# Last MLP product of a decoder block done half by half of the tokens, with a final norm behind each half

## The chip, the cores and the metric

The kernel runs on one core of a Trainium2 chip. The metric is the device time of one execution in microseconds; the kernel before takes 736.61 us, the median of 3 runs (735.38 to 737.58). Engines are called as in the profile: PE is TensorE (PEld its weight loads), DVE is VectorE, ACT is ScalarE, POOL is GpSimd, SP issues DMAs.

## The reference, cut to what matters

One decoder block on 512 tokens of width 1024 in float32: a pooling branch and a differential attention branch, gated and projected; cross attention to 256 memory rows; and a squared-ReLU MLP of width 4096. The change touches only the end:

```
hm = rms_norm(x, g_mlp)
x = x + jnp.square(jax.nn.relu(hm @ w_up)) @ w_down
return rms_norm(x, g_final)
```

`rms_norm(x, g)` is `x * rsqrt(mean(x*x) + 1e-6) * g`, the mean over the 1024 features of each token.

## The kernel before, in words

Activations lie transposed: features on the 128 partitions, tokens along the row, so the residual stream `res` is 8 tiles of 128 x 512. A float32 product is made of three matmuls of rounded halves (`mm3`, lines 103 to 106): high x high, high x low, low x high. Each weight block of 128 x 1024 is loaded by SP into `wraw` (3 buffers) and split by `split` (lines 109 to 111): ACT casts the high part (`whi`, 3 buffers, or two of the 4 buffers of `mhl`), DVE subtracts to get the low part. `weights` (lines 207 to 215) loads up to 7 blocks ahead and splits up to 4 ahead in this stage; it walks one list of blocks (`add`, lines 137 to 141 and 323 to 328).

The MLP runs in 4 groups of 1024 hidden features. A group has two `up_set` calls (lines 874 to 914) that make the activations `act[0..7]`, each a pair (high, low) of 128 x 512, by seven block products of a Strassen scheme; then 8 products m = 0 to 7 with w_down (lines 926 to 951), each over k = 0 to 7 and added to `res[m]`. `act[4..7]` come from the second `up_set` late: `act[4]` and `act[5]` share the tile pair called x in `up_set`, `act[6]` and `act[7]` the pair y, and tokens 0 to 255 and 256 to 511 of each are written by separate instructions. The products m = 0 and 1 therefore begin with k = 0 to 3 of both, and take k = 6, 7, 4, 5 of both afterwards.

In the last group each m also squares `res[m]` into the sum `ss3` and writes `res[m] * g_final` to `y3` (`finish`, lines 916 to 920). Product m = 7 is made by halves of the tokens (A is 0 to 255, B is 256 to 511; `last_rows`, lines 825 to 852). Four k steps behind each half comes its `norm`: three matmuls sum the squares over partitions into PSUM, ACT takes Ln and Exp, DVE does one Newton step, and DVE and POOL multiply `y3` by the result (`ON_POOL`: four of eight pieces on POOL for A, three for B), each pair of pieces followed by an output DMA on SP.

PE's instructions stand in the order written. A scheduler sets the order of the other engines, and each engine works through its list in order. `acc` is a PSUM tag of two buffers, `sc` one of three, `tr` one of two; a product that takes a buffer waits until the one before in it has been read.

Of the kernel before, what the change touches and what calls it, by code (L numbers as in the profile page):

```python
# [14 lines left out]
ALU = mybir.AluOpType  # L15
# [34 lines left out]
def block_kernel(ctx: ExitStack, tc: tile.TileContext, x0g, xT, memT, wv, wm, wst, wckv, wpool, vecs, csts, outT):  # L50
# [272 lines left out]
    for g in range(NG):  # L323
        for n in (2 * g, 2 * g + 1):
            for name in FIRST_ORDER if n == 0 else ORDER:
                where[n, name] = add((n, name))
        for m in range(KC):
            where["dn", g, m] = add(wm[WDN + KC * g + m])
# [496 lines left out]
    def last_rows(m, o, c):  # L825

        w = c.stop - c.start
        V.tensor_tensor(res[m][:, c], o[:, c], res[m][:, c], op=ALU.add)
        sq = tmp()[:, :w]
        S.activation(sq, res[m][:, c], AF.Square)  # L830
        S.activation(y3[m // 2][:, 1, c], res[m][:, c], AF.Copy, scale=vec[:, G_FINAL + m:G_FINAL + m + 1])

        def norm():
            s = ps("tr", 2)[:, :w]
            nc.tensor.matmul(s, ones, st["sp3"][0][:, c], start=True, stop=False)
            nc.tensor.matmul(s, ones, st["sp3"][1][:, c], start=False, stop=False)
            nc.tensor.matmul(s, one_f, sq, start=False, stop=True)
            r, v, l = tmp()[:, :w], tmp()[:, :w], tmp()[:, :w]
            with tc.high_priority():
                S.activation(l, s, AF.Ln, bias=eps, scale=1.0 / D)  # L840
                S.activation(r, l, AF.Exp, scale=-0.5)
                V.tensor_scalar(v, s, 1.0 / D, EPS, op0=ALU.mult, op1=ALU.add)
                V.tensor_tensor(l, r, r, op=ALU.mult)
                V.scalar_tensor_tensor(l, l, -0.5, v, op0=ALU.mult, op1=ALU.mult)
                V.scalar_tensor_tensor(r, l, 1.5, r, op0=ALU.add, op1=ALU.mult)
            for j in range(KC // 2):
                for i in range(2):
                    eng = G if 2 * j + i in ON_POOL[c.start > 0] else V
                    eng.tensor_tensor(y3[j][:, i, c], y3[j][:, i, c], r, op=ALU.mult)  # L849
                nc.sync.dma_start(outT[:, 2 * j:2 * j + 2, c], y3[j][:, :, c])  # L850

        after(4, norm)
# [63 lines left out]
    def finish(m, o, last):  # L916
        residual(m, o)
        if last:
# [106 lines left out]
```

## Time and profile before

| what | us |
|---|---|
| median of 3 runs (lowest, highest) | 736.61 (735.38, 737.58) |
| the profiled execution's own time | 736.63 |
| its span, first to last instruction | 734.5 |
| PE busy in the span | 706.9 (96%) |
| DVE busy | 512.8 (70%) |
| ACT busy | 392.6 (53%) |
| mean granted TensorE clock | 0.986 |

All rows come from this one execution. 2.13 us of its time lie outside the span. Busy time of PE includes the overlap of one matmul with the next, so the pace of matmuls is read from the distance of their starts. A row of the timeline gives start, duration, engine, line, what is written and read, shapes, and in brackets how long the engine was idle before and what ended that.

### The profile page before, as it was taken

The numbers are of one execution on the slowest core, as the hardware profiler recorded it, in microseconds if no ns is written. First come the engines' busy times: TensorE is split into PE (matmuls) and PEld (weight loads), VectorE is DVE, ScalarE is ACT, GpSimd is POOL, SyncE is SP. The second block draws the span as 40 slices with busy tenths as digits, with TensorE's granted clock in tenths as the row PEclk, the third lists the DMA queues.
The fourth block names the chain that finished last, engine by engine and source line by source line (L and its number), as shares of the span: only waits on it lengthen the run. The fifth ranks groups of instructions, "written<-read, shape, count | busy, mean of one in ns | idle before, by whom it ended". The sixth has DMA issues, their size and how long they took to land.

```text
span 734.5 us, 10275 instructions
## 1 busy us (share of the span) xinstructions
PE 706.9 (96%) x3960; PEld 613.9 (84%) x3960; DVE 512.8 (70%) x797; ACT 392.6 (53%) x641; POOL 72.7 (10%) x66
## 2 busy tenths in 40 slices
PE   8999999999999999999986999999999999999993
PEld 6877888788889888888876988899889988899882
DVE  7597999875988555663688984489455974489426
ACT  7498998676765433443655651356213651256422
POOL 0043112534000000000000001000000001000003
PEclk9999999999999999999997999999999999999997
DMA  8433223143535532115633645365354645314003
GB/s 320 138 115 115 85 75 114 58 150 109 172 104 182 177 139 87 58 58 167 177 87 116 184 159 123 87 173 192 87 114 144 202 133 125 86 58 144 30 1 114
DMA packets 28112, 91.09 MB, mean 124 GB/s; under 512 B 3072, under 2 KB 5120, under 8 KB 28064
## 3 DMA queue, kind: packets, MB, share of 16 engines
q1 hardware_dynamic: 25712, 81.92, 33.8%
q0 software_dynamic: 2352, 8.52, 6.8%
q8 instruction: 31, 0.51, 0.3%
q14 instruction: 17, 0.14, 0.1%
HBM read 86.24 MB, written 2.10 MB: 120 GB/s over the span
## 4 chain that ended last, share of the span: by engine, by line
PE 80%; DVE 7%; DMA 5%; ACT 4%; issue 2%; POOL 0%; SPq 0%; DVEq 0%; POOLq 0%
PE acc L104 16%; PE acc L106 15%; PE acc L105 15%; PE sc L104 9%; PE sc L106 9%; PE sc L105 9%; DMA wraw<-wst 2%; DMA mraw<-wst 2%; DVE wlo L111 1%; ACT tmp L447 1%; DVE mix L849 1%; DMA tmp<-xT 1%; DVE tmp L445 1%; PE sc L386 1%; ACT tmp L417 1%
## 5 line engine op out<-in xcount | busy, mean ns | idle before, releaser
L110 ACT CAST whi<-wraw 128x1024 fp32r<-128x1024 f32 (+1 forms) x98 | 102.4, 1045 | 119.0 <-PE acc L105 51.8
L104 PE MATMUL acc<-xg,whi 128*128 128x512 f32 x400 | 158.2, 396 | 1.0 <-DVE vr L572 1.0
L106 PE MATMUL acc<-xg,wlo 128*128 128x512 f32 x400 | 156.1, 390 | 0.0
L105 PE MATMUL acc<-xg,whi 128*128 128x512 f32 x400 | 155.8, 390 | 0.0
L111 DVE TENSOR_TENSOR wlo<-wraw,whi 128x1024 fp32r<-128x1024 f32 (+1 forms) x98 | 121.4, 1238 | 26.1 <-ACT whi L110 25.7
L106 PEld LDWEIGHTS acc<-xg,wlo 128*128 128x128 f32 x400 | 75.1, 188 | 16.2
L104 PEld LDWEIGHTS acc<-xg,whi 128*128 128x128 f32 x400 | 75.2, 188 | 16.0 <-ACT whi L110 1.3
L105 PEld LDWEIGHTS acc<-xg,whi 128*128 128x128 f32 x400 | 75.2, 188 | 14.6
L572 DVE TENSOR_TENSOR vr<-acc,vr 128x512 f32<-128x512 f32 x41 | 28.3, 690 | 72.8 <-PE acc L106 72.8
L104 PE MATMUL sc<-mix,whi 128*128 128x256 f32 (+1 forms) x192 | 56.5, 294 | 0.0
L106 PE MATMUL sc<-mix,wlo 128*128 128x256 f32 (+1 forms) x192 | 56.2, 293 | 0.0
L105 PE MATMUL sc<-mix,whi 128*128 128x256 f32 (+1 forms) x192 | 56.2, 293 | 0.0
L885 DVE TENSOR_TENSOR tmp<-sc,tmp 128x512 f32<-128x512 f32 x56 | 37.7, 688 | 8.7 <-PE sc L106 8.5
L110 ACT CAST mhl<-wraw 128x1024 fp32r<-128x1024 f32 x22 | 23.2, 1054 | 35.9 <-PE acc L105 22.2
L105 PE MATMUL acc<-xg,mhl 128*128 128x512 f32 x104 | 40.6, 390 | 0.0
L104 PE MATMUL acc<-xg,mhl 128*128 128x512 f32 x104 | 40.5, 389 | 0.0
L106 PE MATMUL acc<-xg,mhl 128*128 128x512 f32 x104 | 40.5, 389 | 0.0
L110 ACT CAST whi<-mraw 128x1024 fp32r<-128x1024 f32 x19 | 20.0, 1051 | 38.3 <-PE acc L105 21.8
L104 PEld LDWEIGHTS sc<-mix,whi 128*128 128x128 f32 x192 | 36.3, 189 | 1.0
L106 PEld LDWEIGHTS sc<-mix,wlo 128*128 128x128 f32 x192 | 36.2, 189 | 1.1
L105 PEld LDWEIGHTS sc<-mix,whi 128*128 128x128 f32 x192 | 36.1, 188 | 1.1
L105 PE MATMUL sc<-s,whi 128*128 128x256 f32 x104 | 30.1, 290 | 4.6 <-DVE s L111 4.6
(270 smaller groups left out, 1661.7 us busy)
## 6 DMA issues: line engine op xcount, KB each, us to landing
wraw<-wm SPq DMA_DIRECT2D x76, 512.0 KB, 3.4
mraw<-wst SPq DMA_DIRECT2D x32, 512.0 KB, 3.4
wraw<-wckv SPq DMA_DIRECT2D x16, 512.0 KB, 3.5
mraw<-wst POOLq DMA_DIRECT2D x8, 512.0 KB, 5.7
wraw<-wst SPq DMA_DIRECT2D x8, 512.0 KB, 3.3
wraw<-wst POOLq DMA_DIRECT2D x8, 512.0 KB, 5.8
s<-s SPq DMA_DIRECT2D x8, 256.0 KB, 3.7
vr<-xT SPq DMA_DIRECT2D x8, 256.0 KB, 5.0
```

The source lines that it names most:

```text
L104: nc.tensor.matmul(o, lh, rh, start=start, stop=False)
L105: nc.tensor.matmul(o, lh, rl, start=False, stop=False)
L106: nc.tensor.matmul(o, ll, rh, start=False, stop=stop)
L110: S.copy(hi, src)
L111: eng.tensor_tensor(lo, src, f(hi), op=ALU.subtract)
L386: nc.tensor.matmul(o[i], xg[k][0][:, tb], wh[:, c], start=k == 0, stop=False)
L417: S.copy(b[32 * (j ^ 1):32 * (j ^ 1) + 32, :], o[32 * j:32 * j + 32, :])
L445: V.tensor_tensor_reduce(e[:, :n], o[:, :n], mask[:, T - n:], -0.125, 3.0e38, ALU.add, ALU.min, mn)
L447: S.activation(e[:, :n], e[:, :n], AF.Exp, bias=mn, scale=-1.0, accum_out=sm[:, c:c + 1])
L572: V.tensor_tensor(t, o, t, op=ALU.add)
L849: eng.tensor_tensor(y3[j][:, i, c], y3[j][:, i, c], r, op=ALU.mult)
L885: V.tensor_tensor(u[new], o, u[old], op=ALU.add)
```

## The change

In the last group all 8 products are made for tokens A first and then again for tokens B, each 256 columns wide, in `acc`, over k = 0 to 7 in plain order. The weight blocks of that group stand twice in the list, so they are loaded and split twice. `ss3` and `y3` are filled by halves. A half's sum of squares is split after m = 6, and `last_norm` runs four k steps into the next half's first product (for B: right at the end). It takes its PSUM tile from `acc` in place of `tr`. The multiplications by the norm are four instructions on DVE per half, each over two pieces at once (2 x 256 columns); POOL has none. The other groups keep their products as they were.

```diff
--- before.py
+++ after.py
@@ -324,8 +324,9 @@
         for n in (2 * g, 2 * g + 1):
             for name in FIRST_ORDER if n == 0 else ORDER:
                 where[n, name] = add((n, name))
-        for m in range(KC):
-            where["dn", g, m] = add(wm[WDN + KC * g + m])
+        for n in range(1 if g < NG - 1 else 2):
+            for m in range(KC):
+                where["dn", g, m, n] = add(wm[WDN + KC * g + m])
 
     def W(*key):
         return weights(where[key])
@@ -822,34 +823,46 @@
     ss3 = sb("ss", [P, T], 1)
     y3 = {}
 
-    def last_rows(m, o, c):
-
-        w = c.stop - c.start
-        V.tensor_tensor(res[m][:, c], o[:, c], res[m][:, c], op=ALU.add)
-        sq = tmp()[:, :w]
-        S.activation(sq, res[m][:, c], AF.Square)
-        S.activation(y3[m // 2][:, 1, c], res[m][:, c], AF.Copy, scale=vec[:, G_FINAL + m:G_FINAL + m + 1])
-
-        def norm():
-            s = ps("tr", 2)[:, :w]
-            nc.tensor.matmul(s, ones, st["sp3"][0][:, c], start=True, stop=False)
-            nc.tensor.matmul(s, ones, st["sp3"][1][:, c], start=False, stop=False)
-            nc.tensor.matmul(s, one_f, sq, start=False, stop=True)
-            r, v, l = tmp()[:, :w], tmp()[:, :w], tmp()[:, :w]
-            with tc.high_priority():
-                S.activation(l, s, AF.Ln, bias=eps, scale=1.0 / D)
-                S.activation(r, l, AF.Exp, scale=-0.5)
-                V.tensor_scalar(v, s, 1.0 / D, EPS, op0=ALU.mult, op1=ALU.add)
-                V.tensor_tensor(l, r, r, op=ALU.mult)
-                V.scalar_tensor_tensor(l, l, -0.5, v, op0=ALU.mult, op1=ALU.mult)
-                V.scalar_tensor_tensor(r, l, 1.5, r, op0=ALU.add, op1=ALU.mult)
-            for j in range(KC // 2):
-                for i in range(2):
-                    eng = G if 2 * j + i in ON_POOL[c.start > 0] else V
-                    eng.tensor_tensor(y3[j][:, i, c], y3[j][:, i, c], r, op=ALU.mult)
-                nc.sync.dma_start(outT[:, 2 * j:2 * j + 2, c], y3[j][:, :, c])
-
-        after(4, norm)
+    def last_norm(c, sp, sq):
+
+        s = acc()[:, :M]
+        nc.tensor.matmul(s, ones, sp[0], start=True, stop=False)
+        nc.tensor.matmul(s, ones, sp[1], start=False, stop=False)
+        nc.tensor.matmul(s, one_f, sq, start=False, stop=True)
+        r, v, l = tmp()[:, :M], tmp()[:, :M], tmp()[:, :M]
+        with tc.high_priority():
+            S.activation(l, s, AF.Ln, bias=eps, scale=1.0 / D)
+            S.activation(r, l, AF.Exp, scale=-0.5)
+            V.tensor_scalar(v, s, 1.0 / D, EPS, op0=ALU.mult, op1=ALU.add)
+            V.tensor_tensor(l, r, r, op=ALU.mult)
+            V.scalar_tensor_tensor(l, l, -0.5, v, op0=ALU.mult, op1=ALU.mult)
+            V.scalar_tensor_tensor(r, l, 1.5, r, op0=ALU.add, op1=ALU.mult)
+        rb = r.unsqueeze(1).broadcast_to([P, 2, M])
+        for j in range(KC // 2):
+            V.tensor_tensor(y3[j][:, :, c], y3[j][:, :, c], rb, op=ALU.mult)
+            nc.sync.dma_start(outT[:, 2 * j:2 * j + 2, c], y3[j][:, :, c])
+
+    def last_group(act):
+
+        for m in range(0, KC, 2):
+            y3[m // 2] = sb("mix", [P, 2, T], 8)
+        for n, c in enumerate((A, B)):
+            half = {k: (hi[:, c], lo[:, c]) for k, (hi, lo) in act.items()}
+            s3 = ss3[:, c]
+            for m in range(KC):
+                w = W("dn", NG - 1, m, n)
+                o = acc()[:, :M]
+                tile_mm(o, w, half)
+                t, sq = res[m][:, c], s3 if m == 0 else tmp()[:, :M]
+                V.tensor_tensor(t, o, t, op=ALU.add)
+                S.activation(sq, t, AF.Square)
+                S.activation(y3[m // 2][:, m % 2, c], t, AF.Copy, scale=vec[:, G_FINAL + m:G_FINAL + m + 1])
+                if 0 < m < KC - 1:
+                    V.tensor_tensor(s3, s3, sq, op=ALU.add)
+                if m == KC - 2:
+                    sp = split_sq(s3, M)
+            after(4, last_norm, c, sp, sq)
+        flush()
 
     def two(t):
         return t.rearrange("p (j t) -> p j t", j=2)
@@ -913,42 +926,26 @@
                 plus("C12", o, "U4")
                 squared_relu(*x, u["C12"], B)
 
-    def finish(m, o, last):
-        residual(m, o)
-        if last:
-            accumulate(ss3, m, res[m])
-            S.activation(y3[m // 2][:, m % 2, :], res[m], AF.Copy, scale=vec[:, G_FINAL + m:G_FINAL + m + 1])
-
     for g in range(NG):
         act, begun = {}, []
         for n in (2 * g, 2 * g + 1):
             up_set(n, act, 4 * (n % 2))
+        if g == NG - 1:
+            last_group(act)
+            continue
         for m in range(KC):
-            last = g == NG - 1
-            w = W("dn", g, m)
-            if last and m % 2 == 0:
-                y3[m // 2] = sb("mix", [P, 2, T], 8)
-            if last and m == KC - 1:
-                st["sp3"] = split_sq(ss3, T)
-                for hf, o in enumerate((ps("sc", 3), ps("sc", 3))):
-                    c = slice(hf * M, (hf + 1) * M)
-                    tile_mm(o[:, c], w, {k: (a[:, c], b[:, c]) for k, (a, b) in act.items()})
-                    last_rows(m, o, c)
-                flush()
+            w = W("dn", g, m, 0)
+            o = acc()
+            if m > 1:
+                tile_mm(o, w, act)
+                residual(m, o)
                 continue
-            if m < 2:
-                o = acc()
-                tile_mm(o, w, act, range(4), True, False)
-                begun.append((o, w))
-                if m == 0:
-                    continue
+            tile_mm(o, w, act, range(4), True, False)
+            begun.append((o, w))
+            if m == 1:
                 for i, (o, w) in enumerate(begun):
                     tile_mm(o, w, act, (6, 7, 4, 5), False, True)
-                    finish(i, o, last)
-                continue
-            o = acc()
-            tile_mm(o, w, act)
-            finish(m, o, last)
+                    residual(i, o)
 
 
 def _mtiles(w):
```

How the engines' lists change, at three places. Numbers behind names tell buffers apart.

PE, the first product of the last group and what follows it: `xg_1115` to `xg_1118` are `act[0..3]`, `xg_1150` and `xg_1151` are high and low of x (`act[4]`, `act[5]`), `xg_1152` and `xg_1153` those of y (`act[6]`, `act[7]`), `mhl_1170` and `mhl_1171` the weights of m = 0, `whi_1176` those of m = 1. Before:

```order
L106 MATMUL acc_1190_6457<-xg_1117_5952,mhl_1171_6306 128x512
L104 MATMUL acc_1193_6474<-xg_1115_5950,whi_1176_6345 128x512
L105 MATMUL acc_1193_6474<-xg_1116_5951,whi_1176_6345 128x512
L106 MATMUL acc_1193_6474<-xg_1115_5950,wlo_1177_6346 128x512
L104 MATMUL acc_1193_6474<-xg_1115_5950,whi_1176_6345 128x512
```

And with the change:

```order
L106 MATMUL acc_1193_6460<-xg_1117_5952,mhl_1171_6306 128x256
L104 MATMUL acc_1193_6460<-xg_1150_6200,mhl_1170_6305 128x256
L105 MATMUL acc_1193_6460<-xg_1151_6201,mhl_1170_6305 128x256
L106 MATMUL acc_1193_6460<-xg_1150_6200,mhl_1171_6306 128x256
L104 MATMUL acc_1193_6460<-xg_1150_6200,mhl_1170_6305 128x256
L105 MATMUL acc_1193_6460<-xg_1151_6201,mhl_1170_6305 128x256
L106 MATMUL acc_1193_6460<-xg_1150_6200,mhl_1171_6306 128x256
L104 MATMUL acc_1193_6460<-xg_1152_6202,mhl_1170_6305 128x256
L105 MATMUL acc_1193_6460<-xg_1153_6203,mhl_1170_6305 128x256
```

After 12 matmuls of m = 0, PE went on to the first half of m = 1 before; now the same product's x and y stand there, twelve matmuls of 256 columns behind the start.

DVE around the norm of A: `vr_460` to `vr_467` are `res[0..7]`, L857 in the changed file is the addition of a product to them, L836 to L839 the Newton step, L842 the multiplications, L111 with 128x1024 the low part of a weight block. With the change:

```order
L857 TENSOR_TENSOR vr_467_1898<-acc_1229_6714,vr_467_1898 128x256
L111 TENSOR_TENSOR wlo_1234_6746<-wraw_1214_6632,whi_1233_6745 128x1024
L111 TENSOR_TENSOR tmp_1225_6705<-ss_797_3653,tmp_1224_6704 128x256
L836 TENSOR_SCALAR tmp_1238_6767<-acc_1236_6762 128x256
L837 TENSOR_TENSOR tmp_1239_6768<-tmp_1237_6766 128x256
L857 TENSOR_TENSOR vr_460_1884<-acc_1235_6749,vr_460_1884 128x256
L838 SCALAR_TENSOR_TENSOR tmp_1239_6768<-tmp_1239_6768,tmp_1238_6767 128x256
L839 SCALAR_TENSOR_TENSOR tmp_1237_6766<-tmp_1239_6768,tmp_1237_6766 128x256
L111 TENSOR_TENSOR wlo_1241_6799<-wraw_1219_6668,whi_1240_6798 128x1024
L842 TENSOR_TENSOR mix_1186_6450<-mix_1186_6450,tmp_1237_6766 128x2x256
```

The low part of a weight block now stands between the last addition of A (`vr_467`) and the low part of the sum of squares (`tmp_1225`), and the addition of B's first product (`vr_460`, reading `acc_1235`) stands behind the start of A's Newton step. Four L842 follow there, and then the addition of B's second product.

ACT at the same place; L834 and L835 are Ln and Exp, L858 the square, L859 the scaled copy. With the change:

```order
L110 CAST whi_1233_6745<-wraw_1214_6632 128x1024
L110 CAST tmp_1224_6704<-ss_797_3653 128x256
L859 ACTIVATE mix_1189_6453<-vr_467_1898,vx_1_67 128x256
L858 ACTIVATE tmp_1230_6739<-vr_467_1898 128x256
L834 ACTIVATE tmp_1239_6768<-acc_1236_6762,vx_1_67 128x256
L835 ACTIVATE tmp_1237_6766<-tmp_1239_6768 128x256
```

The cast of a weight block stands ahead of the cast of the sum of squares, and both ahead of the square of A's last piece.

## Rows read from the trace of the kernel before

**Rows 1.** Stretches of the last group and of other stages: busy us of PE, PEld, DVE, ACT and POOL (with instructions), granted clock, DMA share, GB/s.

```profile
480.00:500.00 20.00, 20.00 (x172) 20.00 (x171) 18.42 (x23) 12.76 (x17) 0.86 (x1) 1.00 0.63 183
671.00:680.70 9.70, 9.70 (x67) 8.96 (x66) 9.70 (x14) 7.13 (x10) 0.00 (x0) 1.00 0.52 168
```

**Rows 2.** The chain of work that ended last, three of its last pieces: start, us, engine, tile, line.

```profile
722.42 3.01 DVE mix L849 x4
725.43 0.33 DVE tmp L842
...
728.53 2.06 DVE mix L849 x3
```

**Rows 3.** Timeline of PE: first matmul of the last group (m = 0), first of m = 1, first of the second part of m = 0; then the first matmul of half A of m = 7, and the first of the norm of A with what follows it.

```profile
676.44 0.40 PE L104 MATMUL acc<-xg,mhl 128*128 128x512 f32 x1
...
679.19 0.39 PE L104 MATMUL acc<-xg,whi 128*128 128x512 f32 x1
...
681.91 0.39 PE L104 MATMUL acc<-xg,mhl 128*128 128x512 f32 x1
...
714.55 0.28 PE L104 MATMUL sc<-xg,whi 128*128 128x256 f32 x1
...
718.87 0.28 PE L835 MATMUL tr<-tmp,ones 128*128 128x256 f32 x1
...
719.66 0.28 PE L105 MATMUL sc<-xg,whi 128*128 128x256 f32 x1
```

**Rows 4.** Timeline of PE in the block products of `up_set`: the first matmuls of two products that stand 24 matmuls apart.

```profile
645.34 0.28 PE L104 MATMUL sc<-s,mhl 128*128 128x256 f32 x1
...
648.17 0.28 PE L104 MATMUL sc<-mix,mhl 128*128 128x256 f32 x1
```

**Rows 5.** Timeline of DVE at the start of the last group. The L111 of xg at 677.10 is the low part of x for A, the one at 680.03 that of y for A; the last row is the addition of product m = 2 to `res[2]`.

```profile
677.10 0.68 DVE L111 TENSOR_TENSOR xg<-tmp,xg 128x512 fp32r<-128x512 f32 x1
677.70 0.68 DVE L885 TENSOR_TENSOR tmp<-sc,tmp 128x512 f32<-128x512 f32 x1
678.30 1.22 DVE L111 TENSOR_TENSOR mhl<-wraw,mhl 128x1024 fp32r<-128x1024 f32 x1
679.43 0.69 DVE L860 SCALAR_TENSOR_TENSOR tmp<-tmp,rstd 128x512 f32<-128x512 f32 x1
680.03 0.69 DVE L111 TENSOR_TENSOR xg<-tmp,xg 128x512 fp32r<-128x512 f32 x1
...
692.99 0.69 DVE L572 TENSOR_TENSOR vr<-acc,vr 128x512 f32<-128x512 f32 x1 [2.75 <-PE acc L106]
```

**Rows 6.** Timeline of ACT: the cast of a weight block in m = 2, then the square and the copy of half A of m = 7.

```profile
692.76 1.05 ACT L110 CAST whi<-wraw 128x1024 fp32r<-128x1024 f32 x1 [3.24 <-PE acc L105]
693.73 0.62 ACT L262 ACTIVATE tmp<-vr 128x512 f32<-128x512 f32 x1
...
718.09 0.42 ACT L830 ACTIVATE tmp<-vr 128x256 f32<-128x256 f32 x1 [0.60 <-DVE vr L828]
718.41 0.49 ACT L831 ACTIVATE mix<-vr,vx 128x256 f32<-128x256 f32 x1
```

**Rows 7.** Timeline of all engines from the last matmul of the last product to the end.

```profile
720.85 0.28 PE L106 MATMUL sc<-xg,wlo 128*128 128x256 f32 x1
...
721.17 0.42 DVE L828 TENSOR_TENSOR vr<-sc,vr 128x256 f32<-128x256 f32 x1
...
721.62 0.42 ACT L830 ACTIVATE tmp<-vr 128x256 f32<-128x256 f32 x1 [0.96 <-DVE vr L828]
...
722.09 0.70 PE L837 MATMUL tr<-tmp,onef 128*128 128x256 f32 x2 [0.73 <-ACT tmp L830]
...
722.56 3.45 POOL L849 TENSOR_TENSOR mix<-mix,tmp 128x256 f32<-128x256 f32 x4 [99.50 <-ACT mix L831]
722.83 0.47 ACT L840 ACTIVATE tmp<-tr,vx 128x256 f32<-128x256 f32 x1 [0.39 <-PE tr L837]
723.34 0.42 ACT L841 ACTIVATE tmp<-tmp 128x256 f32<-128x256 f32 x1
...
726.79 0.42 DVE L845 SCALAR_TENSOR_TENSOR tmp<-tmp,tmp 128x256 f32<-128x256 f32 x1
727.24 3.35 DVE L849 TENSOR_TENSOR mix<-mix,tmp 128x256 f32<-128x256 f32 x5
```

**Rows 8.** DMA issues of the page (KB each, median us to landing), then the output DMAs of line 850 on SP's queue: duration min/median/max in ns, first and last start.

```profile
wraw<-wm SPq DMA_DIRECT2D x76, 512.0 KB, 3.4
...
L850 SPq DMA_DIRECT2D outT<-mix x8: 372/372/420, 723.5 to 731.1; - x8
```

**Rows 9.** Timeline of PE in the cross attention, the longest idle stretch in the trace, and the granted clock there and behind it (the columns of rows 1).

```profile
386.79 0.58 PE L105 MATMUL sc<-s,whi 128*128 128x256 f32 x1 [2.84 <-DVE s L111]
...
393.39 0.42 PE L106 MATMUL sc<-s,wlo 128*128 128x256 f32 x1
...
394.88 0.41 PE L104 MATMUL sc<-s,whi 128*128 128x256 f32 x1
384.00:388.00 4.00, 0.80 (x2) 0.50 (x2) 4.00 (x7) 3.20 (x6) 0.00 (x0) 0.81 0.00 0
...
396.00:398.00 2.00, 2.00 (x14) 1.91 (x14) 1.42 (x2) 1.05 (x1) 0.00 (x0) 0.82 0.00 0
```

**Rows 10.** Waits of PE over the whole span, by who was waited for, the longest outside the cross attention: us in total, times, longest.

```profile
PE sc L443 <- DMA s<-s: 1.6, 1, 1.6
```

## The prediction

> **What bounds the kernel now.** I read the windows first. PE is busy without a gap at full granted clock, while DVE, in the 9.7 us up to 680.7, is busy 9.70 of 9.70 us: at the start of the last group it is the engine that runs late [rows 1]. Then the chain of waits: behind the last product it runs on DVE alone, first through A's four multiplications (3.01 us) and only then through B's Newton step and multiplications [rows 2]. So the kernel is PE's matmuls from end to end, and then a tail of 734.5 - 720.85 = 13.65 us behind the start of the last matmul. Last the timelines around both: a change there is worth what it does to PE's last matmul plus what it does to the tail.
>
> **Pace of the matmuls.** Before, the last group has 7 products of 24 matmuls of 512 columns and two half products of 24 of 256. From 676.44 to 714.55 are 168 matmuls in 38.11 us, 226.8 ns each; from 714.55 to 718.87 are 36 of 256 columns in 4.32 us, 120.0 ns each [rows 3]. Two halves cost 13 ns more than a whole. The change turns 168 wide ones into 336 narrow ones: 336 x 0.1200 - 38.11 = +2.21 us. The other bound is the block products' pace, 24 in 2.83 us or 117.9 ns [rows 4]; then all 384 narrow ones take 45.27 against 38.11 + 48 x 0.1200 = 43.87, +1.40 us. I take 120.0, since those are the same operands (`xg` by half, w_down) a few us later.
>
> **The start of the group.** Before, x and y were first needed 24 wide matmuls behind the start, at 681.91 [rows 3]. With the change y of A is needed by matmul 20 of product 0: 676.44 + 19 x 0.12 = 678.72. Its low part is written by the subtraction that starts at 680.03 and takes 0.69 us, so 680.72 and some 0.04 for the signal [rows 5]. DVE can't be earlier: it comes from an unbroken queue, with a weight block's low part (1.22 us) ahead. Nothing before that point changes in any engine's order. PE waits 680.76 - 678.72 = 2.04 us. x of A is ready at 677.78, before 678.00 where it is needed, and costs nothing. I bound the wait by 1.8 and 2.1 us.
>
> **Inside A.** Each half product lasts 24 x 0.12 = 2.88 us. ACT has per product a cast (0.97 us from its start to the next instruction's), a square (0.33) and a copy (about 0.40), 1.7 us [rows 6]. DVE has an addition (0.35), a low part (1.13, by the distance from 678.30 to 679.43) and an addition to the sum (0.35), 1.8 us [rows 5, 7]. Both fit, so the second splitting is hidden by PE; without that cover it would cost DVE's 8 x 1.13 = 9 us. The 8 more loads of 512 KB come at one per 2.88 us, 182 GB/s. The trace moved 183 GB/s in a stretch where PE was busy 20.00 of 20 us [rows 1], and a load that lands after 3.4 us [rows 8] is issued, by the rotation of the three `wraw` buffers, nearly three us before its block must be there for its cast. I take 0.
>
> **The norm of A inside B.** Let B's first matmul start at 0, A's last at -0.12. ACT's next instruction is the cast of a weight block, which waits for the last use of the old high part. A cast starts some 0.2 us before the addition of the product that frees it (692.76 against 692.99) [rows 5, 6]; for a half that addition comes 0.32 us behind the last matmul's start [rows 7], so at 0.20, and the cast at about 0.03 to 0.08. It ends at 1.13; the cast of the sum follows at 1.03. DVE takes the weight's low part first, 1.16 to 2.29, then the sum's, until 2.71. The norm stands on PE 12 matmuls in, and its second matmul, due at 1.44 + 0.12 = 1.56, needs that: PE waits until 2.76, 1.20 us. Queued behind it is only the rest of B's product 0. The norm's three matmuls themselves took 719.66 - 718.87 - 0.12 = 0.67 us before and take as much now [rows 3]. I bound this wait by 0.7 and 1.5.
>
> **The PSUM tile taken from `acc`.** With two buffers, product 0 of B has one and the norm the other, so product 1 must wait until product 0 has been read. That addition comes 0.32 us behind the last matmul's start, 0.20 behind its end, takes 0.43 and signals: 0.68 us in which PE stands. Ahead of it in DVE's list stands the first part of A's Newton step, which waits for Ln and Exp: Ln starts 0.74 us behind the norm's third matmul at 2.88, Exp 0.51 later [rows 7], so that step is through by about 5.0, and product 0 ends at 2.88 + 0.67 + 1.20 = 4.75, its addition due at 4.95. The two nearly meet; bounds 0.6 and 1.1, taken 0.68. Behind it the weight's low part and four multiplications stand ahead of product 1's addition on DVE; they end some 4.3 us behind B's product 0's addition, and product 3, which waits for it, starts 5.8 behind. Hidden by about 1 us.
>
> **The tail.** The last matmul's start is T. As before: addition T + 0.32, square T + 0.77, third norm matmul T + 1.24, Ln T + 1.98, Exp T + 2.49, over at T + 2.91 [rows 7]. A's multiplications are long gone, so DVE goes on at once: three Newton steps of 0.46 each (from 726.79 to 727.24 is 0.45), multiplications from T + 4.33. A 512-wide DVE instruction follows the next at 0.60 (677.10 to 677.70) and takes 0.69 [rows 5]; four end at T + 6.82. Those of before were 256 wide and took 3.01 for four beside POOL and 3.35 for five, which is why B's Newton step began only at 725.4 [rows 2, 7]. Only one output DMA is then left: it starts at 0.04 and takes 0.38 to issue, and the span ended 734.5 - 731.5 = 3.0 us behind the end of the last issue [rows 8]. End at T + 10.24 in place of T + 13.65: -3.41 us; bounds -3.0 and -3.5. A's outputs leave about 15 us earlier than the end and hide.
>
> **The sum.** +2.21 + 2.04 + 1.20 + 0.68 - 3.41 = +2.72 us on the profiled execution's 736.63, which is the median (736.61) as well: 739.3, slower by 0.37%. What the tail gives, PE more than takes back. With all low ends: 1.40 + 1.8 + 0.7 + 0.6 - 3.5 = +1.0, 737.6; all high ends 2.21 + 2.1 + 1.5 + 1.1 - 3.0 = +3.9, 740.5. Some 0.3% (2.2 us) is what a measurement of this kernel tells from no change, so the boundary is 738.8.
>
> **Rivals.**
> - *The narrow pace is the block products'.* At 117.9 ns the sum is 0.81 lower: 738.5, not slower by the boundary. It decides from about 118.6 ns on. For it speaks that most narrow matmuls of the trace run so; against it that those with these operands ran at 120.0. The Trainium skill (TensorE: Matmul & The Clock Gate, section Back-to-back issue gap) gives N/2.4 + 2.5 ns for a matmul; by it the halves would cost 336 x 0.1092 - 168 x 0.2158 = 0.4 us more than the wholes, and the sum would be 737.5. The trace disagrees: 226.8 and 120.0 against its 215.8 and 109.2.
> - *Not slower: the wait at the start of the group is short.* If VectorE's backlog is worked off earlier, y of A is ready sooner. Its whole price is 2.04: 737.2. It decides from 0.5 us on. Against it: DVE's list up to there is unchanged and had not one idle slot in 9.7 us [rows 1].
> - *The clock falls.* The granted clock fell to half (0.50) at about 386.5, inside an idle stretch of PE of 2.84 us, and came back at about 396.7, some 3.7 us after matmuls ran steadily again at 393.0 [rows 9]. An idle stretch of 1.6 us left it [rows 10]. Here 2.04 us stand between the two. At half, a narrow matmul took 1.49 / 7 = 213 ns, 93 more than at full; 3.7 us hold 17 of them, +1.6 us: 740.9.
> - *Faster.* The tail's 3.41 would have to come with two of the four losses missing; nothing in the rows speaks for that.
>
> **How the numbers follow.** Forecast 739.3: 0.52. Pace: 0.13. Short wait: 0.12. Clock: 0.18. Faster: 0.05. The forecast's own spread leaves about a third of it below 738.8; pace and short wait nearly wholly lie within 0.3%. So faster 0.05, within 0.40, slower 0.55. The range goes from 737.2 (short wait) to 741.2 (clock).
>
> **What the next profile would show.** Right: PE idle of about 2 us in the first product, ended by DVE's low part of `xg`; idle of about 1.2 us before the norm's second matmul and 0.7 before B's second product; narrow starts 120 ns apart; the last group's matmuls some 6 us longer; a tail of 10.2 us behind the last matmul; no POOL work there. Wrong: PE without a gap, a pace under 118.6 ns, casts of w_down blocks that wait for DMA, or a granted clock under 1 in the group.

## The result, and the profile after

The changed kernel takes 740.1 us (median of 8 runs, 738.74 to 741.36), the kernel before in the same session 737.6 (8 runs, 735.38 to 740.41): a ratio of 1.0031, 95% interval 1.0018 to 1.0044. The forecast was 739.3 in the range 737.2 to 741.2, slower by 0.37%. The profiled execution took 739.09 us, 2.46 more than that of before; its span is 737.3 us.

The page of the changed kernel, busy time of the engines and the loads of weight blocks:

```profile
PE 711.0 (96%) x4128; PEld 624.5 (85%) x4128; DVE 522.2 (71%) x818; ACT 403.2 (55%) x664; POOL 66.6 (9%) x59
...
wraw<-wm SPq DMA_DIRECT2D x84, 512.0 KB, 3.3
```

Eight more loads land as soon as those of before [rows 8]. PE's share is the same 96%, so the page does not tell where the time went. The waits of PE from the last group to the end (us in total, times, longest):

```profile
PE acc L105 <- DVE xg L111: 1.6, 1, 1.6
PE acc L830 <- DVE tmp L111: 0.9, 1, 0.9
PE acc L831 <- ACT tmp L858: 0.7, 1, 0.7
```

The first is the wait for y of A, the second the norm's second matmul of A, the third belongs to the tail and was there before [rows 7]. A fourth, before B's second product, is missing. The timeline of PE tells the sizes:

```profile
676.69 0.29 PE L104 MATMUL acc<-xg,mhl 128*128 128x256 f32 x1
...
681.02 0.39 PE L105 MATMUL acc<-xg,mhl 128*128 128x256 f32 x1 [1.59 <-DVE xg L111]
...
703.18 0.28 PE L106 MATMUL acc<-xg,wlo 128*128 128x256 f32 x1
703.39 0.38 PE L829 MATMUL acc<-tmp,ones 128*128 128x256 f32 x1
704.68 0.39 PE L830 MATMUL acc<-tmp,ones 128*128 128x256 f32 x1 [0.90 <-DVE tmp L111]
704.90 0.59 PE L831 MATMUL acc<-tmp,onef 128*128 128x256 f32 x2
...
706.64 0.28 PE L106 MATMUL acc<-xg,wlo 128*128 128x256 f32 x1
706.76 0.28 PE L104 MATMUL acc<-xg,mhl 128*128 128x256 f32 x1
...
726.80 0.28 PE L106 MATMUL acc<-xg,mhl 128*128 128x256 f32 x1
```

A product has 24 matmuls at 0.120 us, 2.88 us. The second product starts at 681.71, so the first lasted 5.02: 2.14 us of waiting. The norm of A stands from 703.30 (0.12 behind the matmul at 703.18) to 705.32 (706.76 less the 12 matmuls that follow it in product 0): 2.02 us, of which 0.67 is its work and 1.35 is waiting. Product 1 of B, at 706.76, follows 0.12 behind the matmul before it: no wait. Nothing else is lost: the group's 384 matmuls are 383 distances of 0.120, 45.96 us, and with 2.14 and 2.02 that is the whole of 50.12.

DVE and ACT at these places; on DVE the low part of y of A first, then what surrounds the norm of A, then the end; on ACT the two casts ahead of the norm:

```profile
680.28 0.68 DVE L111 TENSOR_TENSOR xg<-tmp,xg 128x512 fp32r<-128x512 f32 x1
...
703.07 1.23 DVE L111 TENSOR_TENSOR wlo<-wraw,whi 128x1024 fp32r<-128x1024 f32 x1 [0.58 <-ACT whi L110]
704.21 0.42 DVE L111 TENSOR_TENSOR tmp<-ss,tmp 128x256 fp32r<-128x256 f32 x1
706.04 0.42 DVE L836 TENSOR_SCALAR tmp<-acc 128x256 f32<-128x256 f32 x1 [1.42 <-ACT tmp L834]
...
706.97 0.42 DVE L857 TENSOR_TENSOR vr<-acc,vr 128x256 f32<-128x256 f32 x1
...
709.24 2.49 DVE L842 TENSOR_TENSOR mix<-mix,tmp 128x512 f32<-128x512 f32 x4
711.64 0.42 DVE L857 TENSOR_TENSOR vr<-acc,vr 128x256 f32<-128x256 f32 x1
...
731.12 2.50 DVE L842 TENSOR_TENSOR mix<-mix,tmp 128x512 f32<-128x512 f32 x4
```

```profile
701.99 1.05 ACT L110 CAST whi<-wraw 128x1024 fp32r<-128x1024 f32 x1 [1.11 <-issue]
702.94 0.40 ACT L110 CAST tmp<-ss 128x256 fp32r<-128x256 f32 x1
```

The windows of the last group's start, of A and of the norm of A (busy us of PE, PEld, DVE, ACT and POOL with instructions, granted clock, DMA share, GB/s) show DVE without a free moment at the start, as in [rows 1], PE with 1.3 us less than there, and a granted clock of 1.00 throughout, though PE stands still twice:

```profile
671.00:680.70 9.70, 8.39 (x69) 7.99 (x67) 9.70 (x14) 7.01 (x10) 0.00 (x0) 1.00 0.51 163
676.44:701.50 25.06, 23.43 (x193) 23.03 (x192) 18.45 (x28) 15.85 (x26) 0.00 (x0) 1.00 0.52 169
701.50:708.00 6.50, 5.60 (x44) 5.21 (x43) 4.08 (x9) 4.12 (x8) 0.00 (x0) 1.00 0.48 164
```

In the tail, the multiplications end at 733.62, T + 6.82 with T = 726.80 the last product matmul's start; the span ends at 737.32, T + 10.52 in place of 13.65.

| part, us | predicted | measured |
|---|---|---|
| pace, 336 narrow for 168 wide | +2.21 | +2.2 |
| wait for y of A | +2.04 | +2.14 |
| wait of the norm of A | +1.20 | +1.35 |
| wait for the PSUM tile | +0.68 | 0 |
| tail | -3.41 | -3.13 |
| sum | +2.72 | +2.58 |

The measured sum is of the group (676.69 to 726.80, 50.12 us for 44.41) and the tail. That the group began 0.25 later, and that 1.8 us lie outside the span in place of 2.13, makes the remaining difference to 2.46.

### The profile page after: what moved, and what is told of

It reads as the page before. It is cut to its first block, busy times and chain, and to the rows that moved or that the text cites. A ratio compares the mean times of both kernels' runs of the same rounds, so it can differ in the third digit from the quotient of the medians.

```text
span 737.3 us, 10681 instructions
## 1 busy us (share of the span) xinstructions
PE 711.0 (96%) x4128; PEld 624.5 (85%) x4128; DVE 522.2 (71%) x818; ACT 403.2 (55%) x664; POOL 66.6 (9%) x59
## 4 chain that ended last, share of the span: by engine, by line
PE 79%; DVE 9%; ACT 5%; DMA 4%; issue 2%; POOL 0%; SPq 0%; DVEq 0%; POOLq 0%; ACTq 0%
PE acc L104 16%; PE acc L105 16%; PE acc L106 16%; PE sc L104 9%; PE sc L105 9%; PE sc L106 9%; DMA wraw<-wst 2%; DVE wlo L111 2%; ACT whi L110 1%; ACT tmp L448 1%; DVE tmp L446 1%; DMA wraw<-wv 1%; DMA mraw<-wst 1%; PE sc L387 1%; ACT tmp L418 1%
## 5 line engine op out<-in xcount | busy, mean ns | idle before, releaser
L110 ACT CAST whi<-wraw 128x1024 fp32r<-128x1024 f32 (+1 forms) x102 | 106.6, 1045 | 122.4 <-PE acc L105 49.6
L104 PE MATMUL acc<-xg,whi 128*128 128x512 f32 (+1 forms) x440 | 166.3, 378 | 0.1
L106 PE MATMUL acc<-xg,wlo 128*128 128x512 f32 (+1 forms) x440 | 164.0, 373 | 0.0
L105 PE MATMUL acc<-xg,whi 128*128 128x512 f32 (+1 forms) x440 | 163.7, 372 | 0.0
L111 DVE TENSOR_TENSOR wlo<-wraw,whi 128x1024 fp32r<-128x1024 f32 (+1 forms) x102 | 126.2, 1237 | 28.6 <-ACT whi L110 28.1
L106 PEld LDWEIGHTS acc<-xg,wlo 128*128 128x128 f32 x440 | 82.9, 188 | 14.9
L104 PEld LDWEIGHTS acc<-xg,whi 128*128 128x128 f32 x440 | 83.0, 189 | 14.0 <-ACT whi L110 0.5
L105 PEld LDWEIGHTS acc<-xg,whi 128*128 128x128 f32 x440 | 83.0, 189 | 13.3
L573 DVE TENSOR_TENSOR vr<-acc,vr 128x512 f32<-128x512 f32 x34 | 23.4, 689 | 55.1 <-PE acc L106 55.1
L104 PE MATMUL sc<-mix,whi 128*128 128x256 f32 (+1 forms) x192 | 56.7, 295 | 0.0
L105 PE MATMUL acc<-xg,mhl 128*128 128x512 f32 (+1 forms) x136 | 47.1, 346 | 1.6 <-DVE xg L111 1.6
L110 ACT CAST mhl<-wraw 128x1024 fp32r<-128x1024 f32 x26 | 27.4, 1052 | 38.8 <-PE acc L105 23.4
L104 PE MATMUL acc<-xg,mhl 128*128 128x512 f32 (+1 forms) x136 | 47.1, 346 | 0.0
L106 PE MATMUL acc<-xg,mhl 128*128 128x512 f32 (+1 forms) x136 | 47.0, 345 | 0.0
```

Source lines behind the costliest of these rows:

```text
L104: nc.tensor.matmul(o, lh, rh, start=start, stop=False)
L105: nc.tensor.matmul(o, lh, rl, start=False, stop=False)
L106: nc.tensor.matmul(o, ll, rh, start=False, stop=stop)
L110: S.copy(hi, src)
L111: eng.tensor_tensor(lo, src, f(hi), op=ALU.subtract)
L573: V.tensor_tensor(t, o, t, op=ALU.add)
```

## The experiments

The start of the last group differs from one profile to the next (676.4 to 679.3 over the eleven kernels here, in code that none of them changes), and single times of one kernel lie up to some 2.8 us either side of its median. So the parts are read from each profile as the length of the group (first matmul of its products to the start of the last) and the tail (from there to the end of the span); the ratio of times to the kernel before, where a kernel was timed more than once, stands beside them with its 95% interval.

| kernel | group | tail | sum | time to before (interval) |
|---|---|---|---|---|
| before | 44.41 | 13.65 | 58.06 | 1 |
| changed | 50.12 | 10.52 | 60.64 | 1.0031 (1.0018 to 1.0044) |
| e1_begin | 48.42 | 10.53 | 58.95 | 1.0003 (0.9989 to 1.0016) |
| e2_late_acc | 48.88 | 10.53 | 59.41 | timed once |
| e3_tr_late | 48.77 | 10.53 | 59.30 | 0.9999 (0.9987 to 1.001) |
| e4_no_reload | 48.77 | 10.51 | 59.28 | timed once |
| e5_all | 47.07 | 10.53 | 57.60 | 0.9977 (0.9958 to 0.9996) |
| e6_pool | 50.92 | 12.00 | 62.92 | 1.0078 (1.0051 to 1.0105) |
| h1_4 | 44.41 | 11.87 | 56.28 | 0.9963 (0.9948 to 0.9977) |
| h2_4 | 44.73 | 12.28 | 57.01 | 0.9972 (0.996 to 0.9985) |
| h3_4 | 45.05 | 10.87 | 55.92 | 0.9969 (0.9958 to 0.998) |

Sums and times agree within the intervals for most kernels, not for all: the sum of e3_tr_late is 1.24 us above the kernel before, a ratio of 1.0017, and its interval ends at 1.001; that of h2_4 (0.9986) lies just outside its own. So single savings are shown by the profiles; the times bear out their direction.

### The order of k at the start: e1_begin

Products 0 and 1 of A are interleaved, so that x and y of A are needed later.

```diff
+                elif m == 0:
+                    w1, o, o1 = W("dn", NG - 1, 1, 0), acc()[:, :M], acc()[:, :M]
+                    for ks, f, l in ((range(4), True, False), ((4, 5), False, False), ((6, 7), False, True)):
+                        tile_mm(o, w, half, ks, f, l)
+                        tile_mm(o1, w1, half, ks, f, l)
```

> The changed kernel with another order of k in half A: products 0 and 1 together, k = 0 to 3 of both, then 4 and 5 of both, then 6 and 7 of both. Theory (the wait of 2.1 us in the first product is a real part of the loss): y of A is then needed 36 narrow matmuls or 4.3 us behind the start instead of 2.3, which is when its low part is there, so PE's wait on the low part of xg falls from 1.6 to under 0.3 and the span is 1.8 to 2.1 us under the changed kernel's 737.3: 735.3. Rival (what is saved there comes back in another wait, since VectorE is late anyway): another wait of PE of 1 to 2 us appears within the next two products and the span stays at 737 +- 0.5.

The wait for y is gone and a small one has come in its place, the third product's for the addition of the first:

```profile
PE acc L830 <- DVE tmp L111: 0.9, 1, 0.9
PE acc L831 <- ACT tmp L866: 0.7, 1, 0.7
PE acc L104 <- DVE vr L865: 0.2, 1, 0.2
```

The group is 1.70 us shorter than the changed kernel's. All else is as it was, so this much of the loss came from the plain order of k and not from halves as such. 0.44 stays: product 0's last matmul now starts only 0.71 us before product 1's, and its addition stands behind a low part of `xg` on DVE and starts at 683.80, while the third product was due at 683.92 and starts at 684.27. The span of this profile, 737.1, would fit the expectation's rival; but its group began at 678.17 in place of 676.69, ahead of all that was changed, and the ratio fell from 1.0031 to 1.0003.

### The norm's place and its PSUM tile: e2_late_acc and e3_tr_late

In e2_late_acc the norm stands eight k steps into B in place of four, with its tile still from `acc`; e3_tr_late takes the tile from `tr` as well, as the kernel before did.

```diff
-            after(4, last_norm, c, sp, sq)
+            after(8, last_norm, c, sp, sq)
```

and for e3_tr_late also

```diff
-        s = acc()[:, :M]
+        s = ps("tr", 2)[:, :M]
```

> The changed kernel with the norm eight k steps behind its half, PSUM tile still from acc. It asks which of the two acc buffers B's product 1 takes. My prediction's step (the one product 0 has just filled): the norm's three matmuls cover the addition, PE waits 0.1 us, and the run equals the one with the tile from tr. What the changed kernel's trace suggests (the norm's own tile, because its readers stand before product 0's addition in the program): B's product 1 waits for Ln and the first Newton instruction, which stands behind a weight block's low part, about 2.7 us behind product 0's end less the norm's matmuls: PE waits 1.8 to 2.2 us before B's product 1, and the span is about 2 us longer than with tr.

> The changed kernel with its norm's PSUM tile from the tag tr and the norm eight k steps behind its half instead of four. Theory (the norm of A waits 1.26 us because ScalarE and VectorE put a weight block's split ahead of the split of the sum of squares): at 2.88 us behind B's start that split is over (2.7), so PE's wait for tmp L111 vanishes and the span falls by 1.1 to 1.3 to about 736.1; the tail behind the last matmul stays 10.5. Rival (the later norm puts its Newton step and four multiplications in front of the additions of B's products 1 and 2 and costs as much): PE waits before B's product 2 or 3 by about 1 us, span 737 +- 0.4.

In both the norm's wait is gone and the one for y stays. Waits of PE in e2_late_acc:

```profile
PE acc L105 <- DVE xg L111: 1.6, 1, 1.6
PE acc L831 <- ACT tmp L858: 0.7, 1, 0.7
```

The group of e3_tr_late is 1.35 shorter than the changed kernel's, which is the whole of the norm's wait. The two differ by 0.11, so the tile from `acc` costs next to nothing in either place: of the two readings in the expectation the first came true, and the wait of 1.8 to 2.2 us did not come. Why can be read from DVE and PE. In e2_late_acc (DVE, then PE):

```profile
706.19 0.43 DVE L857 TENSOR_TENSOR vr<-acc,vr 128x256 f32<-128x256 f32 x1 [0.32 <-PE acc L106]
...
708.34 0.42 DVE L836 TENSOR_SCALAR tmp<-acc 128x256 f32<-128x256 f32 x1
```

```profile
706.67 0.39 PE L104 MATMUL acc<-xg,mhl 128*128 128x256 f32 x1
```

Product 1 of B starts 0.05 us behind the end of the addition of product 0 (706.62) and long before the norm's tile is last read (708.34), so it has product 0's buffer; the three norm matmuls have covered that wait on PE. In the changed kernel it is the other way round: product 1 starts at 706.76, before the addition of product 0 has begun (706.97), and there are two buffers, so it has the norm's, whose last reader had run from 706.04 to 706.46. In both runs the tile went to the buffer whose last reader stands first in DVE's list; that this was the rule by which it was chosen is read from these two cases, and no run tests it further. The prediction had it go to product 0's buffer by turn.

### No second load and no second splitting: e4_no_reload

As e3_tr_late, but the weight blocks stand once in the list, and all products of B use the block of m = 7.

```diff
-        for n in range(1 if g < NG - 1 else 2):
+        for n in range(1):
...
-                w = W("dn", NG - 1, m, n)
+                w = w if n else W("dn", NG - 1, m, n)
```

> The changed kernel with the norm's tile from tr and the norm eight k steps late, as in the run with both of these, and without the second load and split of the eight weight blocks: half B uses the block of product 7 for all its products, so its output is not the reference's. Theory (the second loads and splits hide under PE): from the first matmul of the last group to the last of B 48.5 to 48.8 us as with them (48.77), tail 10.5. Rival (8 loads of 512 KB, 8 casts and 8 subtractions cost PE time by holding up additions or by slowing matmuls): the group is shorter by 0.5 us or more, or narrow matmuls start less than 119.5 ns apart in B.

The group is that of e3_tr_late to the hundredth, the tail within 0.02. With the norm eight steps late, eight loads of 512 KB, eight casts and eight low parts cost nothing; PE hides them whole. This does not hold where the changed kernel has its norm: the cast and the low part that stand ahead of the sum's split there belong to the second splitting. In e4_no_reload, without them, the sum's low part is over at 702.58, before A's last matmul (702.90). So the 1.35 us of the changed kernel are, by this reading, what its second splitting costs; an early norm without it was not run.

### Both waits out: e5_all

e1_begin and e3_tr_late in one.

> Both mends together: order of k in half A as products 0 and 1 in turn, norm eight k steps behind its half with its tile from tr. Theory (the losses on PE add up: 2.2 for the narrow pace, 2.1 for the start, 1.26 for the norm, against 3.15 from the tail): only the pace is left, span 737.3 - 2.1 - 1.2 = 734.0, ratio to the kernel before about 0.999, so no change that can be measured. Rival (second loads and splits of the weights cost as well, or the clock is lower for the extra work): span 735 or more.

The two savings add up: 1.70 + 1.35 = 3.05, and the group is 3.05 shorter than the changed kernel's. What is left over before is 2.66, the pace (2.2) and the 0.44 of e1_begin; it stands against 3.12 of the tail. The kernel is faster than before, by 0.46 us by the profiles' sums and by more by the ratio (0.9977), where about 0.999 was expected. Its span is 735.3 and not 734.0, since its group began at 677.71, 1.02 later than the changed kernel's.

### The multiplications alone: h1_4

From the kernel before: products 0 to 6 whole with its order of k, product 7 by halves, tile from `tr`, no block loaded twice; only the multiplications are 512 wide and all on VectorE, and product 7's halves lie in `acc`. `NARROW` is the number of products made by halves (1 here).

```diff
+        for m in range(KC - NARROW):
+            w = W("dn", NG - 1, m, 0)
+            o = acc()
...
+        for n, c in enumerate((A, B)):
+            half = {k: (hi[:, c], lo[:, c]) for k, (hi, lo) in act.items()}
+            for m in range(KC - NARROW, KC):
```

> The kernel before with one part of the change alone: seven products wide, only product 7 by halves, but the multiplications by the norm as four VectorE instructions over two pieces, none on GpSimd. PE's part stays 44.4 us from the group's first matmul to the last of product 7. Theory (the tail's gain comes from two things, the faster multiplications and A's being out of the way): A's multiplications take 2.5 us in place of 3.0 and B's 2.5 in place of 3.35, one DMA issue fewer waits at the end, so the tail is 11.6 to 12.0 in place of 13.65; the rest of the 3.15 (about 1.2 to 1.5) needs A's multiplications earlier. Ratio about 0.9975. Rival (VectorE alone is no faster than VectorE beside GpSimd, the gain was A's early norm only): tail 13.2 or more.

The timeline of DVE in the tail of h1_4, which answers to [rows 2, 7]; its last product matmul starts at 721.44:

```profile
723.01 2.50 DVE L843 TENSOR_TENSOR mix<-mix,tmp 128x512 f32<-128x512 f32 x4
725.43 0.42 DVE L837 TENSOR_SCALAR tmp<-tr 128x256 f32<-128x256 f32 x1
...
727.13 2.50 DVE L843 TENSOR_TENSOR mix<-mix,tmp 128x512 f32<-128x512 f32 x4
```

A's multiplications still stand in front of B's Newton step, but take 2.50 us for all eight pieces, where four took 3.01 beside POOL. The tail is 1.78 us shorter with the group unchanged at 44.41. So 1.78 of the 3.13 that the change gained there can be had by who multiplies and how wide alone, without a price on PE; 1.35 is what the order by halves adds to it, for the 2.2 of its pace and two waits. Which of the two counts, the width or POOL's absence, no run separates. An estimate: VectorE instructions of 256 columns follow each other at 0.34 us where POOL is idle (706.97 to 707.31 in the changed kernel), so eight would take some 2.8 us, against 2.50 by 512 and 3.59 for A's eight beside POOL (722.42 to 726.01 before); most of the gain is then POOL's absence.

### The multiplications undone in the changed kernel: e6_pool

```diff
-            V.tensor_tensor(y3[j][:, :, c], y3[j][:, :, c], rb, op=ALU.mult)
+            for i in range(2):
+                eng = G if 2 * j + i in ON_POOL[c.start > 0] else V
+                eng.tensor_tensor(y3[j][:, i, c], y3[j][:, i, c], r, op=ALU.mult)
```

> The changed kernel with one thing undone: the multiplications of the last norm are again in single pieces of 256 columns, of A four of eight and of B three of eight on POOL. Theory (the tail's gain has two parts, the order, which has A's multiplications done long before the end, and VectorE's 512-wide multiplications): the order's part stays, B's multiplications cost DVE 3.35 us beside POOL as before in place of 2.50, so the tail is 10.52 + 0.85 = 11.4 us (11.2 to 11.7) and the group stays at 50.1 (49.9 to 50.3); the time is about 0.8 us longer than the changed kernel's. Rival (who multiplies does not matter once A's are out of the way): tail 10.5. Second rival (POOL's long pieces end last): tail above 12.

Both parts came out longer than expected. The multiplications and output issues of its tail, and the wait of PE that is new in its group:

```profile
733.23 3.35 DVE L844 TENSOR_TENSOR mix<-mix,tmp 128x256 f32<-128x256 f32 x5
733.34 2.62 POOL L844 TENSOR_TENSOR mix<-mix,tmp 128x256 f32<-128x256 f32 x3 [19.59 <-DVE tmp L839]
734.26 3.23 SPq L845 DMA_DIRECT2D outT<-mix  x4
```

```profile
PE acc L104 <- DVE vr L859: 0.5, 1, 0.5
```

In the tail, 0.85 is the multiplications' (3.35 for 2.50), as expected, and they begin 0.13 later behind the last matmul's start (4.45 for 4.32). I had left out that two outputs become ready close together, so that the last issue ends 0.91 behind the last multiplication (737.49 against 736.58) and not 0.44: 0.47 more. The span ends 3.29 behind the last issue, 0.03 more. POOL ends at 735.96 and isn't what ends last, so the second rival is out too, though the tail, 12.00, is as long as it said. Seen from this side, the multiplications are worth 1.48 us of the tail and the order alone 13.65 - 12.00 = 1.65; with the 1.78 of h1_4 the two parts overlap by 0.30. In the group, A's four multiplications on DVE take 3.60 us beside POOL in place of 2.49 and stand ahead of product 1's addition; product 3 of B needs that buffer and starts 0.70 late (714.41, 0.82 behind the matmul before it). The changed kernel had 0.46 to spare there: that addition ends at 712.06, product 3 is due at 706.76 + 2 x 2.88 = 712.52. By the profiles' sums e6_pool is 2.28 us longer than the changed kernel; its ratio says more, some 3.5 us, and the last group in its profile also began 1.2 later than the changed kernel's. Whether that is more than the usual wandering stays open.

### Fewer narrow products: h2_4 and h3_4

As h1_4, but with the last 2 or 3 products by halves, first all of A's and then all of B's, and the sum of squares split by halves.

> Products 0 to 5 wide with the order of k of the kernel before, products 6 and 7 by halves (A6, A7, B6, B7) with the changed kernel's norm, its tile from tr, no block loaded twice. Theory (the pace costs 13 ns per pair of halves, so 0.31 us for one product more by halves; the tail is that of the changed kernel unless A's multiplications stand in front of B7's addition on VectorE): they end about 8 us behind A's end while B7's addition is due at 6.6, so the tail is 11.5 to 12.0, the group 44.7: 56.2 to 56.7 in all, 1.4 to 1.9 under the 58.06 of the kernel before. Rival (the tail needs the whole half B between the norms): tail 13 or more.

> The same with products 5, 6 and 7 by halves. Theory: group 44.4 + 2 x 0.31 = 45.0, A's multiplications over (8 us behind A's end) before B7's addition (9.5), tail 10.5 to 10.7: 55.6 in all, 2.4 under the kernel before; ratio 0.9965 to 0.997. Rival (waits of PE on the norm's operands or on PSUM buffers eat it): group 46 or more, ratio 0.999 or more.

Each narrow product costs 0.32 more on PE (44.41, 44.73, 45.05), as two halves cost 13 ns x 24 more than a whole. The tails go up and then down. DVE of h2_4, whose last product matmul starts at 722.20:

```profile
721.11 2.49 DVE L843 TENSOR_TENSOR mix<-mix,tmp 128x512 f32<-128x512 f32 x4
723.51 0.42 DVE L112 TENSOR_TENSOR tmp<-ss,tmp 128x256 fp32r<-128x256 f32 x1
723.85 0.42 DVE L854 TENSOR_TENSOR vr<-acc,vr 128x256 f32<-128x256 f32 x1
```

A's multiplications now run into the end of B's last product: its addition, due at 722.52, comes at 723.85. DVE of h3_4, last product matmul at 724.37:

```profile
720.40 2.49 DVE L843 TENSOR_TENSOR mix<-mix,tmp 128x512 f32<-128x512 f32 x4
...
724.69 0.42 DVE L854 TENSOR_TENSOR vr<-acc,vr 128x256 f32<-128x256 f32 x1 [0.55 <-PE acc L107]
725.03 0.41 DVE L112 TENSOR_TENSOR tmp<-ss,tmp 128x256 fp32r<-128x256 f32 x1
```

There they are over in time. What keeps this tail 0.35 above 10.52 is the sum's low part, which stands behind the last addition, so that the norm's second matmul waits. Both kernels came out longer than expected, h2_4 at 57.01 for 56.2 to 56.7 and h3_4 at 55.92 for 55.6: the place of the sum's low part on DVE was left out. One more product by halves was worth 1.41 us of tail for 0.32 of pace; the other five that the change makes by halves buy little. h1_4, h2_4 and h3_4 beat the kernel before, by 0.3 to 0.4%, and can't be told apart by their times; by the sums h3_4 is best, 2.14 below before.

## Why the prediction was right, and where not

- **What bounds the kernel, and that the tail's gain is paid back on PE: right.** e5_all shows it by taking the two waits out: the sign turns.
- **Pace: right, at the value chosen.** From 698.26 to 702.94 are 39 distances of 120.0 ns. The rival of the block products' pace falls; why those ran at 117.9, no run here shows. The Trainium skill (TensorE: Matmul & The Clock Gate, section Back-to-back issue gap) gives 109.2 ns for 256 columns as the gap of an isolated matmul, and about 131 ns at 512 columns for a stream of weight loads and matmuls. The prediction took the isolated figure for a stream's. The trace agrees with neither: 120.0 here, 226.8 at 512 columns before.
- **Wait for y: right, 2.14 for 2.04.** e1_begin removes it, so the k order is shown to be its cause, and the rival of a short wait falls. The 0.1 too much comes behind the stop: the first distance, from 681.02 to 681.24, is 0.22 and not 0.12, with no wait in the profile that would explain it. The same 0.1 stands behind the stop at the norm (704.68 to 704.90).
- **Inside A at nothing: right.** The seven products of A behind the first take 7 x 2.88 us, from 681.71 to 701.86, and e4_no_reload shows the second loads hidden. What the second splitting does cost stands in the next term.
- **Norm of A: right in mechanism (the weight block's cast and low part stand in front), 1.35 for 1.20.** e3_tr_late gets back just that much. The order on ACT and DVE is the predicted one; the low part of the sum ended at 704.63, 1.33 behind 703.30, where the prediction had 2.71 - 1.44 = 1.27. The other 0.09 is the longer distance behind the stop.
- **The PSUM tile from `acc`: wrong.** "With two buffers, product 0 of B has one and the norm the other, so product 1 must wait until product 0 has been read." It took the norm's buffer and waited for nothing. The size was not what was wrong: had it taken product 0's, it would have had to wait for the addition that ended at 707.39, and with the 0.05 us from there to the matmul that e2_late_acc shows it would have started 0.68 late. In e2_late_acc it does take product 0's, and loses only 0.1, since the norm's matmuls stand in between. The predicted order of DVE, with the first part of the Newton step ahead of the addition, was right, and by the reading of the two runs above it is just this that made the norm's buffer the earlier one.
- **The tail: right up to the last multiplication (T + 6.82 predicted and measured), 0.28 short behind it.** Of this, 0.02 is in the last issue. The other term was "3.0 us behind the end of the last issue", taken from outputs that were issued further apart. Here the four issues follow each other at 0.60:

The queue of SP in the changed kernel's tail (ends at 734.06, and the span 3.26 later), and the share and rate of the DMA engines from 731.89 to 737.3 in 40 slices of 0.135 us:

```profile
731.89 2.17 SPq L843 DMA_DIRECT2D outT<-mix  x4
```

```profile
DMA  0000002999999999999999999999940200000000
GB/s 0 0 0 0 0 0 98 341 356 303 333 363 341 303 318 379 363 364 296 318 371 348 356 333 341 348 341 341 356 144 0 61 0 0 0 0 0 0 0 0
```

And in the kernel before from 728.28 to 734.5, slices of 0.156 us:

```profile
DMA  0000019999869999300019999999996000000000
GB/s 0 0 0 0 0 53 329 349 356 323 244 204 342 356 356 336 126 0 0 0 46 336 316 329 389 336 329 342 369 342 224 13 0 0 0 0 0 0 0 0
```

At some 340 GB/s an output of 262,144 bytes takes 0.77 us, so four at 0.60 pile up: the engines are busy without a pause until about 735.95, some 1.9 behind the end of the last issue (the 61 further on is a packet of 8 KB of the instruction queue). Before there was a pause, and the last transfer was over at about 733.15, some 1.65 behind. That is about 0.25, the term's error. h1_4, which issues at the same distance, ends 3.24 behind its last issue. But e6_pool, whose issues have the pause of the kernel before and whose transfers end some 1.7 behind the last issue, still ends 3.29 behind it. So the piling up accounts for the changed kernel's 0.25, and is not all that moves this term; what else does stays open. A's outputs are issued from 709.95 on, over 25 us before the end and not 15, which changes nothing.

- **Clock: the rival fell.** The two stops, 2.14 us lost at y of A and 1.35 at the norm, left the granted clock at 1.00. The prediction set 2.04 us of lateness beside the 1.6 and 2.84 us of [rows 9, 10], which are idle times; as idle time the stop at y was 1.59, no longer than the 1.6 of [rows 10]. (2.84 is also not the longest in that trace: 3.13 us, up to 390.72, came when the clock was already at 0.50.) The range's upper end, 741.2, is 0.3 above what the clock's own sum gave, 740.9.

The two misses, 0.68 too much and 0.28 too little, and the two slightly larger waits nearly cancel, so it is luck that the sum came out within 0.14 us of the prediction; that the pace, the two waits and the tail's order came out as reasoned is not. That the time is slower by about 0.3% lies right at what a measurement can tell; the interval of the ratio, 1.0018 to 1.0044, leaves out 1.

## What to carry to other kernels

Before a whole last stage is cut in halves for a shorter tail, ask how much of the tail is the order and how much the width and engine of the last instructions: here the latter alone gave 1.78 us where the whole change gave 3.13, at no price on PE, and three products by halves gave most of the remainder for 0.64 of pace, where eight cost 2.2 and two waits. What a half needs first, its operands and the split of its sum, must be ready when PE gets there: look at what stands in front of them on the engine that makes them. And before a wait for a buffer is priced, ask which buffer it will be: here it was the one whose last reader stood first in the reading engine's list, not the next in turn.

## What the runs showed of the hardware that was not expected

A VectorE multiplication of 128 x 256 took 0.94 us beside POOL and 0.41 without it, one of 128 x 512 alone 0.69. The group rows of the multiplications in the kernel before (duration min/median/max in ns, first and last start) show it, as VectorE and POOL come out nearly alike:

```profile
L849 DVE TENSOR_TENSOR mix<-mix,tmp x9: 410/939/945, 722.4 to 730.2; 128x256 f32<-128x256 f32 x9
...
L849 POOL TENSOR_TENSOR mix<-mix,tmp x7: 866/899/964, 722.6 to 729.1; 128x256 f32<-128x256 f32 x7
```

Two engines at work finished A's eight pieces of 256 columns in 3.59 us (722.42 to 726.01), one each 0.45; VectorE alone with 512-wide instructions took 2.50, one each 0.31: the help of POOL made it slower. This fits the Trainium skill (SBUF — State Buffer, section SBUF: two separate sides), by which a VectorE instruction with two SBUF inputs and a GpSimd one that reads SBUF each hold the shared ports for a whole instruction; no run here has POOL's multiplications without VectorE's beside them.

The other surprise is that the outputs' own transfers become the slower part as soon as the multiplications are quick: a pair of pieces is ready every 0.60 us, and its transfer takes 0.77.
